# Encoder layer on one core: the first two column groups of each part's down product computed together

## The chip, the cores and the metric

The kernel runs on one core of one Trainium2 chip. The metric is device time in microseconds (us); lower is better. The engines are called as in the profile: PE (TensorE, matmuls), PEld (its weight loads), DVE (VectorE), ACT (ScalarE), POOL (GpSimd) and SP (SyncE, which here only starts DMA transfers).

## What is computed

One layer of an encoder on 256 tokens with model width 2048 and feed-forward width 5632: a feed-forward block, a mixer of three attention-like groups, a second feed-forward block, each between two RMS norms.

```python
def _swiglu(x, w_gate_up, w_down):
    gu = x @ w_gate_up
    g, u = jnp.split(gu, 2, axis=-1)
    return (jax.nn.silu(g) * u) @ w_down
...
    f = _swiglu(_rmsnorm(h, ffn1_norm_pre[l]), ffn1_w_gate_up[l], ffn1_w_down[l])
    h = h + 0.5 * _rmsnorm(f, ffn1_norm_post[l])
    ...
    f = _swiglu(_rmsnorm(h, ffn2_norm_pre[l]), ffn2_w_gate_up[l], ffn2_w_down[l])
    h = h + 0.5 * _rmsnorm(f, ffn2_norm_post[l])
```

## The kernel before

**Numbers.** Everything is fp32. Each operand of a large product is split into a high and a low part (`split_out` for activations, `load_unit` for weights), and the product is made of three matmuls: high by high, high by low, low by high (lines 221 to 223).

**Weights.** `load_unit` brings one block of 512 rows by 512 columns (1 MB) with one DMA on SP's queue into one of three buffers `raw`, and splits it in two units of 256 rows each: ACT writes `whi` (line 209), DVE writes `wlo` (line 210). There are four buffers of each, so a unit can be split at most four units ahead of PE: unit k needs the buffer of unit k-4 back. `mm_unit` multiplies one unit with one token tile (t is 0 or 1, 128 tokens each): 6 matmuls of 128x512, called a step below. A unit is two steps.

**A feed-forward block** (`ffn`) walks over the 11 chunks of 512 hidden columns in three parts of 4, 4 and 3 chunks. For each chunk it computes gate and up (`gemm` over the whole width), then `turn` transposes the product of both. That is a chain of five: the product on DVE (line 319, `th`), a block transpose on DVE (line 165, `blk`), a DMA out to DRAM (line 167, `blkd`), four DMAs back (line 170, `trn`), both started by POOL, and the split into high and low, `h_aT` on ACT (line 133) and `l_aT` on DVE (line 134), for t=0 and then t=1. After the last chunk of a part, `gemm` computes the down product of the part's chunks for each of four groups of 512 columns (oc 0 to 3), and `done` adds it to the rows F. The chunks are used in order, so within oc 0 the chunk that was made last comes last, 12 steps after the end of gate and up in a part of 4 chunks, 8 steps after it in a part of 3. The prediction calls the parts F1-0, F1-1, F1-2 (first block) and F2-0, F2-1, F2-2 (second).

**Side work.** `later(delay, ...)` puts work into a list that is emptied as steps pass (or earlier, when a product needs it): the splits of a chunk come 8 and 9 steps after its `turn`. `beside_down` is called after a column group of the first block. At (1, 0) it loads the memory rows and puts a small product (`spread`, `ps_d`) 8 steps later; in part 2 it loads and splits one piece of the memory, transposed (`rawT`, `h_mT`, `l_mT`), per column group.

**Order.** PE and SP run in the order in which the code is written. On ACT, DVE and POOL a scheduler sets the order when the program is built, and each of these engines then runs its instructions in that fixed order.

Of the kernel before, what the change touches and what calls it, by code (L numbers as in the profile page):

```python
# [9 lines left out]
F32 = mybir.dt.float32  # L10
F32R = mybir.dt.float32r
AF = mybir.ActivationFunctionType
ALU = mybir.AluOpType
# [3 lines left out]
P = 128  # L17
T = 256
NT = T // P
D = 2048  # L20
FF = 5632
CH = 512
KG = 4
# [18 lines left out]
def encoder_layer(ctx: ExitStack, tc: tile.TileContext, x, xt, mem, memt, f1_gu, f1_dn, f2_gu, f2_dn, w_in, w_kv, w_out,  # L42
                  cols, bias, ws_t, rows, out):
    nc = tc.nc
# [11 lines left out]
    psum = ctx.enter_context(tc.tile_pool(name="psum", bufs=8, space=PS))  # L56
# [23 lines left out]
    step = [0]  # L80
# [5 lines left out]
    def run_side(pair=None, t=None):  # L86

        n = sum(1 for e in side if e[0] <= step[0])
        if pair is not None:
            for i, e in enumerate(side):  # L90
                if e[2] is pair and (t is None or e[3] is None or e[3] == t):
                    n = max(n, i + 1)
        for _ in range(n):
            side.pop(0)[1]()
# [101 lines left out]
    def load_unit(w, k0, nk, c0, fine=False):  # L196

        raw = wraw.tile([P, KG, CH], F32, name="raw", tag="raw")
        src = w[c0 // CH, k0 // KG][:, k0 % KG:k0 % KG + nk, :]
        for j in range(0, nk, 1 if fine else nk):  # L200
            e = j + 1 if fine else nk
            nc.sync.dma_start(out=raw[:, j:e, :], in_=src[:, j:e, :])
        got = []
        for j in range(0, nk, 2):
            hi = wsp.tile([P, 2, CH], F32R, name="whi", tag="whi")
            lo = wsp.tile([P, 2, CH], F32R, name="wlo", tag="wlo")
            for i in range(0, 2, 1 if fine else 2):
                a, b = slice(i, i + 1 if fine else 2), slice(j + i, j + i + 1 if fine else j + 2)
                nc.scalar.copy(out=hi[:, a, :], in_=raw[:, b, :])  # L209
                nc.vector.tensor_tensor(out=lo[:, a, :], in0=raw[:, b, :], in1=hi[:, a, :].bitcast(F32), op=ALU.subtract)  # L210
            got.append((hi, lo))
        return got

    def mm_unit(ps, t, pair, half, w, first, last):
        hi, lo = pair
        whi, wlo = w
        ts = slice(t * P, (t + 1) * P)
        for j in range(2):
            kt = 2 * half + j
            f, l = first and j == 0, last and j == 1  # L220
            nc.tensor.matmul(ps, lhsT=hi[:, kt, ts], rhs=whi[:, j, :], start=f, stop=False)  # L221
            nc.tensor.matmul(ps, lhsT=hi[:, kt, ts], rhs=wlo[:, j, :], start=False, stop=False)  # L222
            nc.tensor.matmul(ps, lhsT=lo[:, kt, ts], rhs=whi[:, j, :], start=False, stop=l)  # L223

    def gemm(pairs, w, k0, c0, skew_in=False, skew_out=False, feed=None, nk=KG, done=None):

        ps = [psum.tile([P, CH], F32, name=f"pg{t}", tag="ps") for t in range(NT)]
        n = 2 * len(pairs)  # L230
        units = []
        order = [(u, t) for u in range(n) for t in range(NT)]
        S = min(4, n)
        if skew_in:
            order = [(u, t) for t in range(NT) for u in range(S)] + [(u, t) for u, t in order if u >= S]
        if skew_out:
            order = [(u, t) for u, t in order if u < n - S] + [(u, t) for t in range(NT) for u in range(n - S, n)]
        for u, t in order:
            while len(units) <= u:
                if feed:  # L240
                    feed(len(units))
                units += load_unit(w, k0 + 2 * len(units), nk, c0, nk < KG and len(units) < 2)
            run_side(pairs[u // 2], t)
            mm_unit(ps[t], t, pairs[u // 2], u % 2, units[u], u == 0, u == n - 1)
            if done and u == n - 1:
                done(t, ps[t])
            step[0] += 1
            run_side()
        return ps

    def gemm_T(pairs, w, c0, done):

        ps = [psum.tile([P, CH], F32, name=f"pT{h}", tag="ps")[:, 0:T] for h in range(4)]
        n = 2 * len(pairs)
        units = []
        order = [(u, h) for u in range(n - 2) for h in range(4)] + [(u, h) for h in range(4) for u in (n - 2, n - 1)]
        for i, (u, h) in enumerate(order):
            while len(units) <= u:
                units += load_unit(w, 2 * len(units), KG, c0)
            pair = pairs[u // 2]  # L260
            run_side(pair)
            hi, lo = pair
            whi, wlo = units[u]
            hs = slice(h * P, (h + 1) * P)
            for j in range(2):
                kt = 2 * (u % 2) + j
                f, l = u == 0 and j == 0, u == n - 1 and j == 1
                nc.tensor.matmul(ps[h], lhsT=whi[:, j, hs], rhs=hi[:, kt, :], start=f, stop=False)  # L268
                nc.tensor.matmul(ps[h], lhsT=whi[:, j, hs], rhs=lo[:, kt, :], start=False, stop=False)  # L269
                nc.tensor.matmul(ps[h], lhsT=wlo[:, j, hs], rhs=hi[:, kt, :], start=False, stop=l)  # L270
            if u == n - 1:
                done(h, ps[h])
            if i % 2:
                step[0] += 1
                run_side()
# [9 lines left out]
    def row_scale(src):  # L285

        return [rsqrt_mean(sum_cols(square_sums([src[:, t, q * CH:(q + 1) * CH] for q in range(4)])), D)
                for t in range(NT)]

    def ffn(trn, xT, w_gu, w_dn, F, on_last, feeds=None, beside_down=None):  # L290
        half_r, rr = [], []
        n_ch = FF // CH
        parts = [range(0, 4), range(4, 8), range(8, 11)]
        for ip, part in enumerate(parts):
            aT = []
            for c in part:
                feed_g, feed_u = feeds if c == 0 and feeds else (None, None)
                g = gemm(xT, w_gu, 0, c * CH, skew_in=(c == 0 and not feeds), feed=feed_g, nk=2 if feed_g else KG)
                u = None
                if feed_u:  # L300
                    u = gemm(xT, w_gu, 0, FF + c * CH, feed=feed_u)
                if c == 0:
                    for r in row_scale(H):
                        a = small.tile([P, 1], F32, name="half_r", bufs=4)
                        b = small.tile([P, 1], F32, name="rr2", bufs=4)
                        nc.vector.tensor_scalar_mul(a, r, 0.5)
                        nc.vector.tensor_tensor(out=b, in0=a, in1=r, op=ALU.mult)
                        half_r.append(a)
                        rr.append(b)
                s = []  # L310
                for t in range(NT):
                    th = tmp.tile([P, CH], F32, name="th", tag="tmp")
                    nc.scalar.activation(out=th, in_=g[t], func=AF.Tanh, scale=half_r[t])
                    nc.vector.scalar_tensor_tensor(out=th, in0=th, scalar=1.0, in1=g[t], op0=ALU.add, op1=ALU.mult)
                    s.append(th)
                u = u or gemm(xT, w_gu, 0, FF + c * CH)
                pair = act_pair("aT")
                for t in range(NT):
                    nc.vector.scalar_tensor_tensor(out=s[t], in0=s[t], scalar=rr[t], in1=u[t], op0=ALU.mult,
                                                   op1=ALU.mult)  # L320
                split = turn(trn, s, pair)
                for t in range(NT):
                    later(8 + t, lambda split=split, t=t: split(t), pair, t)
                aT.append(pair)
            last = ip == len(parts) - 1
            for oc in range(4):

                def done(t, d):
                    f = F[t][:, oc * CH:(oc + 1) * CH]

                    def add():
                        nc.vector.tensor_tensor(out=f, in0=f, in1=d, op=ALU.add)

                    if ip == 0:
                        nc.scalar.copy(out=f, in_=d)
                    elif not last:
                        add()
                    else:
                        on_last(oc, t, f, add)

                gemm(aT, w_dn, part[0] * KG, oc * CH, skew_out=last and oc == 3, done=done)
                if beside_down:
                    beside_down(ip, oc)

# [28 lines left out]
    F = token_rows("F")  # L373
# [44 lines left out]
    with tc.tile_pool(name="trn1", bufs=1) as trn:  # L418
        ffn(trn, xT, f1_gu, f1_dn, F, lambda oc, t, f, add: (add(), post[0].piece(oc, t, f)), feeds=(first_xT, first_rows),
            beside_down=memory_T)  # L420
# [370 lines left out]
```

## Time and profile before

| | |
|---|---|
| time, median of 3 runs | 1861.13 us (1861.03, 1861.13, 1865.01) |
| time of the profiled execution | 1863.18 us |
| its span, first to last instruction | 1861.4 us |
| PE busy | 1820.2 us (98%) |
| DVE, ACT, POOL busy | 1077.2, 867.6, 83.3 us |
| DMA moved | 382.35 MB, 205 GB/s over the span |

The rows that follow come from the profiled execution. Busy time of PE is that of overlapping matmuls: one matmul of 128x512 shows as 0.39 us, but the next one starts 0.227 us after it, so distances are read from start to start. "Granted clock" is the share of PE's full speed (2.4 GHz) that the chip allowed; the lower level is 1.2 GHz.

### The profile page before, as it was taken

Reading aid. Unit: us, or ns where it says so; the run is one execution under the profiler, and the core shown is the slowest. Engines: PE = TensorE matmul, PEld = TensorE weight load, DVE = VectorE, ACT = ScalarE, POOL = GpSimd, SP = SyncE. Lnnn points to the kernel's source line nnn. Section 1 sums busy time; section 2 is a strip of 40 time slices with the busy share of each in tenths; the row PEclk is TensorE's granted clock in tenths of the full one; section 3 lists DMA queues with packets and bytes.
Section 4 is the critical chain, followed back from the end, with each engine's and each line's share of the span. In section 5 each row is a group of like instructions: output and inputs, shape, how many; then the busy total and the mean of one; then the engine's idle time right before and its main releaser. Section 6 shows DMA issues by size and latency. Waiting matters only on the chain.

```text
span 1861.4 us, 21799 instructions
## 1 busy us (share of the span) xinstructions
PE 1820.2 (98%) x8662; PEld 1527.8 (82%) x8662; DVE 1077.2 (58%) x1228; ACT 867.6 (47%) x1096; POOL 83.3 (4%) x139
## 2 busy tenths in 40 slices
PE   9999999999999979999999999999999999999986
PEld 7888888888888868999999877888888887888875
DVE  6555445555455556856765776555445555455556
ACT  6444444445344434645454556444444443344444
POOL 0000000000000000000000000001000000000000
PEclk9999999999999989999999999999999999999998
DMA  8666655667556664554554545666556666556652
GB/s 322 242 207 225 204 196 205 224 213 269 182 202 205 239 194 181 204 181 160 208 191 177 191 180 205 210 224 221 205 195 213 221 208 214 194 196 211 224 183 90
DMA packets 63957, 382.35 MB, mean 205 GB/s; under 512 B 8048, under 2 KB 10096, under 8 KB 22256
## 3 DMA queue, kind: packets, MB, share of 16 engines
q1 hardware_dynamic: 51120, 347.10, 52.8%
q0 software_dynamic: 7392, 23.08, 4.5%
q10 hardware_dynamic: 5344, 10.79, 1.7%
q8 instruction: 67, 1.10, 0.2%
q14 instruction: 34, 0.28, 0.0%
HBM read 367.31 MB, written 13.63 MB: 205 GB/s over the span
## 4 chain that ended last, share of the span: by engine, by line
PE 87%; DMA 5%; issue 3%; DVE 3%; ACT 1%; POOL 1%; SPq 0%; POOLq 0%; ACTq 0%; DVEq 0%
PE pg L221 26%; PE pg L223 26%; PE pg L222 26%; PE pT L270 2%; PE pT L268 2%; PE pT L269 2%; DMA trn<-blkd 2%; DMA blkd<-blk 1%; DMA raw<-in_f_gu 1%; DMA memrow<-in_mem 1%; DVE H L369 1%; DVE wlo L210 1%; POOL trn L170 1%; ACT junk L123 1%; ACT whi L209 0%
## 5 line engine op out<-in xcount | busy, mean ns | idle before, releaser
L210 DVE TENSOR_TENSOR wlo<-raw,whi 128x1024 fp32r<-128x1024 f32 (+1 forms) x650 | 791.8, 1220 | 686.5 <-ACT whi L209 685.4
L209 ACT CAST whi<-raw 128x1024 fp32r<-128x1024 f32 (+1 forms) x650 | 681.8, 1050 | 840.3 <-PE pg L223 777.8
L222 PE MATMUL pg<-wlo,h_xT 128*128 128x512 f32 x1408 | 548.8, 390 | 2.2 <-DVE wlo L210 2.2
L221 PE MATMUL pg<-whi,h_xT 128*128 128x512 f32 x1408 | 549.1, 390 | 0.9 <-ACT h_xT L133 0.8
L223 PE MATMUL pg<-whi,l_xT 128*128 128x512 f32 x1408 | 548.3, 389 | 0.5 <-DVE l_xT L134 0.5
L222 PEld LDWEIGHTS pg<-wlo,h_xT 128*128 128x128 f32 x1408 | 264.4, 188 | 59.3 <-DVE wlo L210 4.4
L221 PEld LDWEIGHTS pg<-whi,h_xT 128*128 128x128 f32 x1408 | 264.4, 188 | 56.5 <-ACT whi L209 1.3
L223 PEld LDWEIGHTS pg<-whi,l_xT 128*128 128x128 f32 x1408 | 264.4, 188 | 56.3 <-DVE l_xT L134 1.3
L221 PE MATMUL pg<-whi,h_aT 128*128 128x512 f32 x704 | 276.4, 393 | 18.4 <-ACT h_aT L133 18.4
L223 PE MATMUL pg<-whi,l_aT 128*128 128x512 f32 x704 | 275.6, 391 | 0.0
L222 PE MATMUL pg<-wlo,h_aT 128*128 128x512 f32 x704 | 275.5, 391 | 0.0
L221 PEld LDWEIGHTS pg<-whi,h_aT 128*128 128x128 f32 x704 | 133.1, 189 | 47.7 <-ACT h_aT L133 20.5
L223 PEld LDWEIGHTS pg<-whi,l_aT 128*128 128x128 f32 x704 | 133.0, 189 | 29.7 <-DVE l_aT L134 2.0
L222 PEld LDWEIGHTS pg<-wlo,h_aT 128*128 128x128 f32 x704 | 133.1, 189 | 27.5
L268 PE MATMUL pT<-h_hT,whi 128*128 128x256 f32 x320 | 91.0, 284 | 0.0
L270 PE MATMUL pT<-h_hT,wlo 128*128 128x256 f32 x320 | 90.5, 283 | 0.0
L269 PE MATMUL pT<-l_hT,whi 128*128 128x256 f32 x320 | 90.5, 283 | 0.0
L167 POOL DMA_DIRECT2D blkd<-blk x22 | 12.9, 587 | 1096.4 <-DVE blk L165 1070.3
L269 PEld LDWEIGHTS pT<-l_hT,whi 128*128 128x128 f32 x320 | 61.4, 192 | 0.2
L268 PEld LDWEIGHTS pT<-h_hT,whi 128*128 128x128 f32 x320 | 61.4, 192 | 0.2
L270 PEld LDWEIGHTS pT<-h_hT,wlo 128*128 128x128 f32 x320 | 61.4, 192 | 0.0
L170 POOL DMA_DIRECT2D trn<-blkd x88 | 53.0, 631 | 86.8 <-DMA blkd<-blk 65.5
(160 smaller groups left out, 1252.3 us busy)
## 6 DMA issues: line engine op xcount, KB each, us to landing
raw<-in_f_gu SPq DMA_DIRECT2D x172, 1024.0 KB, 4.8
raw<-in_f_dn SPq DMA_DIRECT2D x88, 1024.0 KB, 4.8
raw<-in_w_in SPq DMA_DIRECT2D x36, 1024.0 KB, 4.8
raw<-in_w_out SPq DMA_DIRECT2D x16, 1024.0 KB, 4.9
blkd<-blk POOLq DMA_DIRECT2D x22, 512.0 KB, 3.3
trn<-blkd POOLq DMA_DIRECT2D x88, 128.0 KB, 5.5
raw<-in_w_kv SPq DMA_DIRECT2D x8, 1024.0 KB, 4.8
grow<-in_rows ACTq DMA_DIRECT2D x4, 1024.0 KB, 6.0
```

What stands on the lines that cost most here:

```text
L123: nc.scalar.activation(out=junk, in_=src, func=AF.Square, accum_out=acc)
L167: nc.gpsimd.dma_start(out=d, in_=b)
L170: nc.gpsimd.dma_start(out=c[q * B:(q + 1) * B].rearrange("i t (a c) -> i t a c", a=KG), in_=d[:, :, q * P:(q + 1) * P].rearrange("(a i) t ...
L209: nc.scalar.copy(out=hi[:, a, :], in_=raw[:, b, :])
L210: nc.vector.tensor_tensor(out=lo[:, a, :], in0=raw[:, b, :], in1=hi[:, a, :].bitcast(F32), op=ALU.subtract)
L221: nc.tensor.matmul(ps, lhsT=hi[:, kt, ts], rhs=whi[:, j, :], start=f, stop=False)
L222: nc.tensor.matmul(ps, lhsT=hi[:, kt, ts], rhs=wlo[:, j, :], start=False, stop=False)
L223: nc.tensor.matmul(ps, lhsT=lo[:, kt, ts], rhs=whi[:, j, :], start=False, stop=l)
L268: nc.tensor.matmul(ps[h], lhsT=whi[:, j, hs], rhs=hi[:, kt, :], start=f, stop=False)
L269: nc.tensor.matmul(ps[h], lhsT=whi[:, j, hs], rhs=lo[:, kt, :], start=False, stop=False)
L270: nc.tensor.matmul(ps[h], lhsT=wlo[:, j, hs], rhs=hi[:, kt, :], start=False, stop=l)
L369: nc.vector.scalar_tensor_tensor(out=H[:, t, c], in0=self.f[t, q], scalar=self.r[t], in1=H[:, t, c], op0=ALU.mult, op1=ALU.add)
```

## The change

A new function `gemm_pair` computes the down products of column groups 0 and 1 together, in four PSUM tiles (two column groups by two token tiles). It goes through all chunks but the last for group 0, through all but the last for group 1, then through the last chunk for group 0 and for group 1. Groups 2 and 3 stay as they were. `beside_down(ip, 0)` and `(ip, 1)` are both called after the pair. The number of instructions of each kind stays the same.

```diff
--- before.py
+++ after.py
@@ -247,6 +247,22 @@
             step[0] += 1
             run_side()
         return ps
+
+    def gemm_pair(pairs, w, k0, cols, done):
+
+        ps = [[psum.tile([P, CH], F32, name=f"pg{t}", tag="ps") for t in range(NT)] for _ in cols]
+        n = 2 * len(pairs)
+        for us in (range(0, n - 2, 2), range(n - 2, n, 2)):
+            for g, c0 in enumerate(cols):
+                for u0 in us:
+                    for u, unit in enumerate(load_unit(w, k0 + 2 * u0, KG, c0), u0):
+                        for t in range(NT):
+                            run_side(pairs[u // 2], t)
+                            mm_unit(ps[g][t], t, pairs[u // 2], u % 2, unit, u == 0, u == n - 1)
+                            if u == n - 1:
+                                done(g, t, ps[g][t])
+                            step[0] += 1
+                            run_side()
 
     def gemm_T(pairs, w, c0, done):
 
@@ -323,22 +339,27 @@
                     later(8 + t, lambda split=split, t=t: split(t), pair, t)
                 aT.append(pair)
             last = ip == len(parts) - 1
-            for oc in range(4):
-
-                def done(t, d):
-                    f = F[t][:, oc * CH:(oc + 1) * CH]
-
-                    def add():
-                        nc.vector.tensor_tensor(out=f, in0=f, in1=d, op=ALU.add)
-
-                    if ip == 0:
-                        nc.scalar.copy(out=f, in_=d)
-                    elif not last:
-                        add()
-                    else:
-                        on_last(oc, t, f, add)
-
-                gemm(aT, w_dn, part[0] * KG, oc * CH, skew_out=last and oc == 3, done=done)
+
+            def done(oc, t, d):
+                f = F[t][:, oc * CH:(oc + 1) * CH]
+
+                def add():
+                    nc.vector.tensor_tensor(out=f, in0=f, in1=d, op=ALU.add)
+
+                if ip == 0:
+                    nc.scalar.copy(out=f, in_=d)
+                elif not last:
+                    add()
+                else:
+                    on_last(oc, t, f, add)
+
+            gemm_pair(aT, w_dn, part[0] * KG, (0, CH), done)
+            if beside_down:
+                beside_down(ip, 0)
+                beside_down(ip, 1)
+            for oc in (2, 3):
+                gemm(aT, w_dn, part[0] * KG, oc * CH, skew_out=last and oc == 3,
+                     done=lambda t, d, oc=oc: done(oc, t, d))
                 if beside_down:
                     beside_down(ip, oc)
 
```

The first place is **PE in part F1-0**, at the point where all but the last chunk have been used for column group 0. In a name like `h_aT_1416` the number tells buffers apart: 516, 816 and 1116 (low parts 517, 817, 1117) are the first three chunks of the part, 1416 the last; `pg0_1430` and `pg1_1431` are group 0's PSUM tiles, `pg0_1432` and `pg1_1433` group 1's. Before:

```order
L221 MATMUL pg1_1431<-whi_1508,h_aT_1116 128x512
L222 MATMUL pg1_1431<-wlo_1509,h_aT_1116 128x512
L223 MATMUL pg1_1431<-whi_1508,l_aT_1117 128x512
L221 MATMUL pg0_1430<-whi_1540,h_aT_1416 128x512
L222 MATMUL pg0_1430<-wlo_1541,h_aT_1416 128x512
L223 MATMUL pg0_1430<-whi_1540,l_aT_1417 128x512
```

With the change:

```order
L221 MATMUL pg1_1431<-whi_1510,h_aT_1116 128x512
L222 MATMUL pg1_1431<-wlo_1511,h_aT_1116 128x512
L223 MATMUL pg1_1431<-whi_1510,l_aT_1117 128x512
L221 MATMUL pg0_1432<-whi_1542,h_aT_516 128x512
L222 MATMUL pg0_1432<-wlo_1543,h_aT_516 128x512
L223 MATMUL pg0_1432<-whi_1542,l_aT_517 128x512
```

The last chunk's first use moved from 72 matmuls behind the start of the down product to 144 behind it (in a part of 3 chunks from 48 to 96).

The second place is **ACT in part F1-2**, around the split of the last chunk (`h_aT_4692`). The two `whi` of one `raw` are two units; in both kernels 4708 or 4710 holds units 0 and 1, 4778 or 4780 units 4 and 5. Before (4838 holds units 6 and 7, 4872 units 8 and 9):

```order
L209 CAST whi_4840<-raw_4838 128x1024
L209 CAST whi_4844<-raw_4838 128x1024
L133 CAST h_aT_4692<-trn_4701 128x4x128 x2
L133 CAST h_mT_4822<-rawT_4824 128x512
L133 CAST h_mT_4822<-rawT_4830 128x512
L133 CAST h_mT_4948<-rawT_4950 128x512
L133 CAST h_mT_4948<-rawT_4956 128x512
L133 CAST h_mT_5074<-rawT_5076 128x512
L133 CAST h_mT_5074<-rawT_5082 128x512
L133 CAST h_mT_5200<-rawT_5202 128x512
L184 DMA rawT_5208<-in_memt 128x512
L209 CAST whi_4874<-raw_4872 128x1024
```

With the change (4850 holds units 8 and 9, 4892 units 10 and 11):

```order
L209 CAST whi_4852<-raw_4850 128x1024
L133 CAST h_aT_4692<-trn_4701 128x4x128 x2
L133 CAST h_mT_4934<-rawT_4936 128x512
L133 CAST h_mT_4934<-rawT_4942 128x512
L209 CAST whi_4856<-raw_4850 128x1024
L133 CAST h_mT_4948<-rawT_4950 128x512
L133 CAST h_mT_4948<-rawT_4956 128x512
L133 CAST h_mT_5074<-rawT_5076 128x512
L209 CAST whi_4894<-raw_4892 128x1024
L133 CAST h_mT_5074<-rawT_5082 128x512
L133 CAST h_mT_5200<-rawT_5202 128x512
L184 DMA rawT_5208<-in_memt 128x512
```

The split of the last chunk stands one unit later than before, behind unit 8, and the splits of the memory pieces, which stood in one run before the next unit, now stand in groups before units 9, 10 and 11.

The third place is **DVE in the same part**, from the last weight unit ahead of the last chunk's low part. Before:

```order
L210 TENSOR_TENSOR wlo_4845<-raw_4838,whi_4844 128x1024
L134 TENSOR_TENSOR l_aT_4693<-trn_4701,h_aT_4692 128x4x128 x2
L134 TENSOR_TENSOR l_mT_4823<-rawT_4824,h_mT_4822 128x512
L134 TENSOR_TENSOR l_mT_4823<-rawT_4830,h_mT_4822 128x512
L134 TENSOR_TENSOR l_mT_4949<-rawT_4950,h_mT_4948 128x512
L134 TENSOR_TENSOR l_mT_4949<-rawT_4956,h_mT_4948 128x512
L134 TENSOR_TENSOR l_mT_5075<-rawT_5076,h_mT_5074 128x512
L134 TENSOR_TENSOR l_mT_5075<-rawT_5082,h_mT_5074 128x512
L134 TENSOR_TENSOR l_mT_5201<-rawT_5202,h_mT_5200 128x512
L210 TENSOR_TENSOR wlo_4875<-raw_4872,whi_4874 128x1024
```

With the change:

```order
L210 TENSOR_TENSOR wlo_4853<-raw_4850,whi_4852 128x1024
L134 TENSOR_TENSOR l_aT_4693<-trn_4701,h_aT_4692 128x4x128 x2
L134 TENSOR_TENSOR l_mT_4935<-rawT_4936,h_mT_4934 128x512
L134 TENSOR_TENSOR l_mT_4935<-rawT_4942,h_mT_4934 128x512
L210 TENSOR_TENSOR wlo_4857<-raw_4850,whi_4856 128x1024
L134 TENSOR_TENSOR l_mT_4949<-rawT_4950,h_mT_4948 128x512
L134 TENSOR_TENSOR l_mT_4949<-rawT_4956,h_mT_4948 128x512
L210 TENSOR_TENSOR wlo_4895<-raw_4892,whi_4894 128x1024
L134 TENSOR_TENSOR l_mT_5075<-rawT_5076,h_mT_5074 128x512
L134 TENSOR_TENSOR l_mT_5075<-rawT_5082,h_mT_5074 128x512
L134 TENSOR_TENSOR l_mT_5201<-rawT_5202,h_mT_5200 128x512
L210 TENSOR_TENSOR wlo_4899<-raw_4892,whi_4898 128x1024
```

The order is that of ACT: two, two and three low parts of the memory pieces stand ahead of the low parts of units 9, 10 and 11. In the parts of 4 chunks the split of the last chunk keeps its place, behind unit 8 and ahead of unit 9.

## Rows read from the trace of the kernel before

**Rows 1.** The page: span, PE's busy time, and granted clock in 40 slices (tenths).

```profile
span 1861.4 us, 21799 instructions
...
PE 1820.2 (98%) x8662; PEld 1527.8 (82%) x8662; DVE 1077.2 (58%) x1228; ACT 867.6 (47%) x1096; POOL 83.3 (4%) x139
...
PEclk9999999999999989999999999999999999999998
```

**Rows 2.** PE's waits on the last chunk: us in total, times, longest us.

```profile
PE pg L221 <- ACT h_aT L133: 18.4, 5, 11.4
```

**Rows 3.** Timeline of PE, part F1-0: start us, duration us, instruction, [idle before].

```profile
184.59 0.39 PE L221 MATMUL pg<-whi,h_aT 128*128 128x512 f32 x1
...
200.69 0.39 PE L223 MATMUL pg<-whi,l_aT 128*128 128x512 f32 x1
...
202.84 0.40 PE L221 MATMUL pg<-whi,h_aT 128*128 128x512 f32 x1
```

**Rows 4.** Timeline of PE, around the waits in F1-1 and F2-1.

```profile
463.07 0.39 PE L223 MATMUL pg<-whi,l_aT 128*128 128x512 f32 x1
...
464.71 0.40 PE L221 MATMUL pg<-whi,h_aT 128*128 128x512 f32 x1
...
1569.84 0.39 PE L223 MATMUL pg<-whi,l_aT 128*128 128x512 f32 x1
...
1572.21 0.39 PE L221 MATMUL pg<-whi,h_aT 128*128 128x512 f32 x1
```

**Rows 5.** Timeline of PE, around the wait in F1-2.

```profile
676.47 0.39 PE L223 MATMUL pg<-whi,l_aT 128*128 128x512 f32 x1
...
688.30 0.79 PE L221 MATMUL pg<-whi,h_aT 128*128 128x512 f32 x1 [11.44 <-ACT h_aT L133]
...
693.45 0.40 PE L221 MATMUL pg<-whi,h_aT 128*128 128x512 f32 x1
```

**Rows 6.** Timeline of PE, around the wait in F2-2.

```profile
1783.49 0.39 PE L223 MATMUL pg<-whi,l_aT 128*128 128x512 f32 x1
...
1789.01 0.79 PE L221 MATMUL pg<-whi,h_aT 128*128 128x512 f32 x1 [5.13 <-ACT h_aT L133]
...
1792.50 0.39 PE L223 MATMUL pg<-whi,l_aT 128*128 128x512 f32 x1
```

**Rows 7.** Windows of F1-2: busy us by engine, then granted clock, DMA share, GB/s.

```profile
677.00:688.00 11.00, 0.00 (x0) 0.00 (x0) 1.23 (x1) 1.31 (x2) 2.33 (x4) 0.62 0.76 209
688.00:693.50 5.50, 5.20 (x13) 4.05 (x14) 5.22 (x9) 4.40 (x9) 0.00 (x0) 0.52 0.14 49
```

**Rows 8.** Timelines of POOL, ACT and DVE in F1-2.

```profile
668.43 0.58 POOL L167 DMA_DIRECT2D blkd<-blk  x1 [37.28 <-DVE blk L165]
...
676.92 2.41 POOL L170 DMA_DIRECT2D trn<-blkd  x4 [7.91 <-DMA blkd<-blk]
...
676.89 1.04 ACT L209 CAST whi<-raw 128x1024 fp32r<-128x1024 f32 x1 [1.62 <-PE pg L223]
...
687.63 1.14 ACT L133 CAST h_aT<-trn 128x512 fp32r<-128x512 f32 x2 [9.69 <-DMA trn<-blkd]
...
688.67 1.65 ACT L133 CAST h_mT<-rawT 128x512 fp32r<-128x512 f32 x3
...
677.97 1.23 DVE L210 TENSOR_TENSOR wlo<-raw,whi 128x1024 fp32r<-128x1024 f32 x1 [1.44 <-ACT whi L209]
...
688.28 1.29 DVE L134 TENSOR_TENSOR l_aT<-trn,h_aT 128x512 fp32r<-128x512 f32 x2 [9.08 <-ACT h_aT L133]
...
689.49 4.30 DVE L134 TENSOR_TENSOR l_mT<-rawT,h_mT 128x512 fp32r<-128x512 f32 x7
```

**Rows 9.** Timeline of ACT: the last chunk's split in F2-1 and F2-2.

```profile
1570.48 1.14 ACT L133 CAST h_aT<-trn 128x512 fp32r<-128x512 f32 x2 [1.88 <-DMA trn<-blkd]
...
1788.34 1.14 ACT L133 CAST h_aT<-trn 128x512 fp32r<-128x512 f32 x2 [3.38 <-DMA trn<-blkd]
```

**Rows 10.** Windows, columns as in Rows 7: 128x256 matmuls over four open PSUM tiles.

```profile
749.50:757.50 8.00, 8.00 (x69) 8.00 (x69) 7.56 (x11) 5.52 (x12) 1.46 (x1) 1.00 0.99 386
```

## The prediction

> **What bounds the kernel now.** I read the page first. PE is busy for 1820.2 of 1861.4 us, and the granted clock is at 9 tenths or more in all but two slices, of which one is the 15th of 40 (651 to 698 us, with the start of F1-2's down product in it) and the other the last [rows 1]. So PE is the bound nearly everywhere, and a change that neither adds nor removes matmuls can only win or lose in PE's pauses and in the stretches at the lower clock. The table of PE's waits came second. Nearly all of what PE waits for has one cause, the split of a part's last chunk: 18.4 us in five waits, the longest 11.4 us [rows 2]. Third I went to the timeline of PE at each of these waits and measured the whole loss from start to start, because what is lost is more than the idle time.
>
> The pitch without a wait: from the first to the 72nd matmul of the down product in F1-0 there are 71 distances in 200.69 - 184.59 = 16.10 us, 0.2268 us each [rows 3]. A step of 6 matmuls is then 1.36 us, a unit 2.72 us. The loss of each wait is the distance from the last matmul ahead of it to the first one back in rhythm, less the pitch of the matmuls between:
> - F1-0: 202.84 - 200.69 = 2.15, less 4 pitches (0.91): 1.24 us [rows 3]
> - F1-1: 464.71 - 463.07 = 1.64, less 0.91: 0.73 us [rows 4]
> - F2-1: 1572.21 - 1569.84 = 2.37, less 0.91: 1.46 us [rows 4]
> - F1-2: 693.45 - 676.47 = 16.98, less 13 pitches (2.95): 14.03 us [rows 5]
> - F2-2: 1792.50 - 1783.49 = 9.01, less 9 pitches (2.04): 6.97 us [rows 6]
>
> Together 24.4 us; F2-0 has no such wait. The two parts of 3 chunks make 21.0 of it. In F1-2, 688.30 - 676.47 - 0.23 = 11.6 us are the wait itself, and 2.4 us follow it: the 12 matmuls from 688.30 to 693.45 start 0.43 us apart in place of 0.23 [rows 5], and the window shows a granted clock of 0.52, the lower of the two levels, behind a stretch in which PE ran nothing [rows 7]. F2-2 has the same on a smaller scale, 5.3 and 1.7 us.
>
> **What the change removes.** It lets PE do 72 or 48 matmuls more before the last chunk is needed: 144 matmuls (32.7 us) after the start of the down product in a part of 4, 96 (21.8 us) in a part of 3. Against this stands when the split really comes. I count from the start of the down product, found by going back from the last matmul ahead of the wait (71 or 47 pitches).
> - Parts of 4: the latest is F2-1. It starts at 1569.84 - 16.10 = 1553.74, and the split starts at 1570.48 [rows 9], 16.7 us in. Wanted at 32.7: 16 us to spare. The whole loss goes, 1.24 + 0.73 + 1.46 = 3.4 us.
> - F2-2: start 1783.49 - 10.66 = 1772.83, split at 1788.34 [rows 9], 15.5 us in, wanted at 21.8: 6 us to spare. 6.97 us go.
> - F1-2: start 676.47 - 10.66 = 665.81. The split starts at 687.63, and PE's first matmul with it at 688.30, 22.5 us in [rows 5, 8]. Wanted at 21.8. So here a wait of 0.7 us stays. The chain is slow in this part: between the DMA out at 668.43 and the DMAs back at 676.92 lie 8.5 us, of which POOL waits 7.9 [rows 8]. Nothing that the change touches runs ahead of 676.47, and from there to the split the same transfers are queued, since ACT stands at the split and frees no further `raw`; so I let the chain end where it did.
>
> **What is late next.** ACT and DVE keep a fixed order, and the split waits on them ahead of later weight units. In the parts of 4 it stands between units 8 and 9. In F2-1 ACT would be through with it at 16.7 + 1.14, `whi` of unit 9 takes 1.04 and its `wlo` 1.23 [rows 8, 9]: ready 20.2 us in. PE reaches unit 9 after 108 matmuls, 24.5 us in. So 4 us of cover are left, and a later split would cost PE from there on what it is late, no matter that the chunk itself is wanted only at 32.7. In F2-2 (15.5 us in) there is more.
>
> F1-2 has no such cover, and the memory pieces stand in the way as well. On ACT an `h_mT` takes 1.65 / 3 = 0.55 us, on DVE an `l_mT` 4.30 / 7 = 0.61 us [rows 8]. With the split where it was:
> - third matmul of unit 8: half of `l_aT` is done at 688.28 + 0.65 = 688.93, wanted at 688.75; I take 0.3 us with the loads behind it
> - unit 9: ACT 688.67 + 2 x 0.55 + 1.04 = 690.8; DVE behind two `l_mT` and 1.23 of its own 692.05; PE wants it at 665.81 + 108 pitches + 1.0 + 0.23 = 691.5: 0.5 us late
> - unit 10: DVE 694.75, PE wants it at 694.77: just in time
> - unit 11: DVE 694.75 + 3 x 0.61 + 1.23 = 697.8, wanted at 697.5: 0.3 us late
>
> So F1-2 keeps 0.7 + 0.3 + 0.5 + 0.3 = 1.8 us of its 14.0. The pauses are short ones, like those of the parts of 4, after which the matmuls were back at full pitch within four [rows 3, 4], so I add nothing for the clock.
>
> **What I cost at nothing.** Matmuls, weight blocks, POOL's and SP's instructions stay the same in number. The two groups' adds (and in the last parts the gains behind them) come closer together: eight operations of 128x512, some 0.65 us each as half of `l_aT` [rows 8], 5.2 us, beside four `wlo` (4.9 us), in four units of PE (10.9 us). DVE holds that with little to spare; what covers it is that the units are split up to four ahead. If that cover is gone, as it may be in F1-2 behind the late split, it costs up to 2 us. The four open PSUM tiles instead of two: see the third rival. The memory's side product moves by one column group, with its inputs ready as before.
>
> **Sum.** 24.4 - 1.8 = 22.6 us. The profiled execution took 1863.18 us (1861.4 of it its span), which gives 1840.6. The median of the runs is 2.05 us lower. The waits end with DMA landings, which is what may differ between runs: if the 2 us lie there, the new kernel has 1840.6 in every run; if elsewhere, 1838.6. I take 1839.8, and the bounds: all 24.4 gone on the lower runs 1836.7; a split in F1-2 that is later by as much as F1-2 is behind F2-2 today (22 - 15.5 = 6.5 us) 1847.1.
>
> **Rivals.**
> 1. *The wait moves to the weights behind the split.* If the split comes later with PE running on (the DMAs back now share their time with busy matmuls), F1-2 pays each us in full, and units 9 to 11 stack up behind it. For it: ACT and DVE stand still in front of the split today, with 1.3 and 1.2 us of work in 11 [rows 7]. Against it: the weights wanted in that time are split already. [...] 3 to 9 us: 1843 to 1850. Chance 0.11.
> 2. *Nothing is gained*, because something else fills the pauses, DMA above all: its engines are 0.76 busy in the pause of F1-2 [rows 7]. Then PE would wait for `whi` or `wlo` instead. But these waits would have to be as long as the old ones, and a unit, on which PE works 2.72 us, costs ACT and DVE only 1.04 and 1.23 us [rows 8]. 1858 to 1864. Chance 0.03.
> 3. *Slower: the clock falls while four PSUM tiles are open.* The place is the pair, 4 x 192 + 2 x 144 = 1056 matmuls. At the lower level each costs 0.20 us more [rows 5], 211 us if all did; from 113 of them on (11%) the gain of 22.6 us is gone, and from 131 on the kernel is measurably slower, 1865 us or more. Against it: today's transposed products go round four open tiles, 69 matmuls of half the width in 8.00 us, 0.116 us each, at a granted clock of 1.00 [rows 10], and the pair changes between two tiles at a time as before. Chance 0.03. The Trainium skill speaks for this rival (TensorE: Matmul & The Clock Gate, "A second HAM failure mode: psum-queue depth-cycling"): cycling through PSUM banks made TensorE pause so often between groups of matmuls that its clock went back and forth between the levels. This trace has no sign of it with four tiles; by that rule the sum would be a loss, by the row it is nothing.
>
> **How the numbers follow.** The forecast, 1836.5 to 1843, has 0.80. Rival 1 has 0.11, rivals 2 and 3 have 0.03 each, and 0.03 is left for a time below 1836.5, if PE gains more than its waits. The range goes from 1836 to 1847: it holds the forecast and the nearer half of rival 1. A measurement of this kernel can tell about 0.2% (3.7 us) from no change. Faster than that are the forecast, what lies below it and rival 1, 0.94; same 0.03; slower 0.03.
>
> **What would show it.** PE's waits on the last chunk's split are gone but for some 1 us in F1-2. There `whi` and `wlo` of units 9 and 11 appear as new waits of under 1 us each. The granted clock is full in the 15th slice. In F2-1 the split still starts some 17 us into the down product, and unit 9 is split by 20 us. The prediction is wrong if the split of F1-2 starts more than 25 us into the down product, if PE waits for weights in the parts of 4, or if matmuls of the pair start more than 0.23 us apart.

## The result and the profile after

The changed kernel takes 1839.34 us (median of 4 runs, 1838.24 to 1840.51), the kernel before 1862.51 us on the same chip (4 runs, 1861.03 to 1865.01). The ratio is 0.9874, 95% interval 0.9857 to 0.9891: 1.26% faster. The profiled executions took 1863.18 us before and 1840.51 us after, 22.7 us apart.

The page after the change, with the same three rows as in [rows 1]:

```profile
span 1838.7 us, 21801 instructions
...
PE 1815.0 (99%) x8662; PEld 1526.4 (83%) x8662; DVE 1076.3 (59%) x1228; ACT 866.3 (47%) x1096; POOL 83.5 (5%) x139
...
PEclk9999999999999999999999999999999999999998
```

PE is busy for 5.2 us less (most of it the matmuls at the lower clock, which were longer), in a span that is 22.7 us shorter, and the granted clock no longer drops in the 15th slice. All of PE's waits after the change (us in total, times, longest us):

```profile
PE pg L222 <- DVE wlo L210: 2.2, 5, 0.8
PE pt L144 <- DVE H L390: 1.9, 2, 1.0
PE warm_ps L75 <- POOL ones L62: 1.1, 1, 1.1
PE pg L221 <- ACT whi L209: 0.8, 1, 0.8
PE pg L221 <- ACT h_xT L133: 0.8, 1, 0.8
PE pg L223 <- DVE l_xT L134: 0.4, 1, 0.4
PE pT L286 <- DVE wlo L210: 0.2, 1, 0.2
```

The row of [rows 2] has no counterpart: nothing on PE waits for `h_aT` by this table. What is left is old work at the start of the kernel and between the blocks, and one new piece, which the timeline of PE in F1-2 shows (start us, duration us, instruction, [idle before]; to be read beside [rows 5]):

```profile
686.04 0.39 PE L223 MATMUL pg<-whi,l_aT 128*128 128x512 f32 x1
686.57 0.50 PE L221 MATMUL pg<-whi,h_aT 128*128 128x512 f32 x1
686.91 0.40 PE L222 MATMUL pg<-wlo,h_aT 128*128 128x512 f32 x1
687.30 0.50 PE L223 MATMUL pg<-whi,l_aT 128*128 128x512 f32 x1
687.64 0.40 PE L221 MATMUL pg<-whi,h_aT 128*128 128x512 f32 x1
...
689.70 0.39 PE L221 MATMUL pg<-whi,h_aT 128*128 128x512 f32 x1
690.36 0.50 PE L222 MATMUL pg<-wlo,h_aT 128*128 128x512 f32 x1 [0.27 <-DVE wlo L210]
690.70 0.40 PE L223 MATMUL pg<-whi,l_aT 128*128 128x512 f32 x1
```

The distance from 686.04 to 686.57 is 0.53 us, one pitch (0.23) and 0.30 of waiting for the split; the three matmuls that follow are 0.39 late together. The distance from 689.70 to 690.36 is 0.66, a wait of 0.43 for `wlo` of unit 9, with 0.11 behind it. These are all distances above the pitch in F1-2: 1.23 us, where [rows 5] had 14.03. The other five parts have none, and over the pair of each part the granted clock is 1.00. The timelines of POOL, ACT and DVE in F1-2, beside [rows 8]:

```profile
667.13 0.58 POOL L167 DMA_DIRECT2D blkd<-blk  x1 [37.26 <-DVE blk L165]
...
675.88 2.41 POOL L170 DMA_DIRECT2D trn<-blkd  x4 [8.18 <-DMA blkd<-blk]
...
685.90 1.14 ACT L133 CAST h_aT<-trn 128x512 fp32r<-128x512 f32 x2 [6.54 <-DMA trn<-blkd]
...
687.99 1.05 ACT L209 CAST whi<-raw 128x1024 fp32r<-128x1024 f32 x1
...
686.55 1.29 DVE L134 TENSOR_TENSOR l_aT<-trn,h_aT 128x512 fp32r<-128x512 f32 x2 [5.93 <-ACT h_aT L133]
...
687.76 1.29 DVE L134 TENSOR_TENSOR l_mT<-rawT,h_mT 128x512 fp32r<-128x512 f32 x2
...
689.08 1.23 DVE L210 TENSOR_TENSOR wlo<-raw,whi 128x1024 fp32r<-128x1024 f32 x1
```

The down product starts at 686.04 - 95 pitches = 664.5. The DMA out is issued 2.6 us in, the DMAs back 11.4 us in, the split starts 21.4 us in; before it was 2.6, 11.1 and 21.8. The chain is what it was, and PE has other work while it runs. In the two parts that [rows 9] show, the split starts at:

```profile
1555.89 1.14 ACT L133 CAST h_aT<-trn 128x512 fp32r<-128x512 f32 x2 [1.52 <-DMA trn<-blkd]
...
1774.56 1.14 ACT L133 CAST h_aT<-trn 128x512 fp32r<-128x512 f32 x2 [2.59 <-DMA trn<-blkd]
```

F2-1 starts at 1539.5 (2.6 us ahead of its DMA out) and F2-2 at 1757.1: 16.4 and 17.4 us in, and wanted at 32.7 and 21.8.

### The profile page after: what moved, and what is told of

Same layout as the page of the kernel before. It is cut to its first block, busy times and chain, and to the rows that moved or that the text cites. A ratio compares the mean times of both kernels' runs of the same rounds, so it can differ in the third digit from the quotient of the medians.

```text
span 1838.7 us, 21801 instructions
## 1 busy us (share of the span) xinstructions
PE 1815.0 (99%) x8662; PEld 1526.4 (83%) x8662; DVE 1076.3 (59%) x1228; ACT 866.3 (47%) x1096; POOL 83.5 (5%) x139
## 4 chain that ended last, share of the span: by engine, by line
PE 93%; DVE 2%; DMA 2%; ACT 1%; POOL 0%; issue 0%; SPq 0%; ACTq 0%; POOLq 0%
PE pg L222 28%; PE pg L223 28%; PE pg L221 28%; PE pT L286 2%; PE pT L284 2%; PE pT L285 2%; DMA raw<-in_f_gu 1%; DVE H L390 1%; DVE wlo L210 1%; DMA H<-in_x 1%; DMA trn<-blkd 0%; DMA blkd<-blk 0%; ACT whi L209 0%; ACT junk L123 0%; PE ps_p L528 0%
```

## Experiments

For each run I give the loss in the six down products, measured start to start as in the prediction (24.5 us in the profiled execution before, with 0.1 us in F2-0). The time of an execution less this loss should be the same number for every kernel with the same work, if these losses are all that differs.

### The pair in the parts of 3 chunks only

```diff
-            gemm_pair(aT, w_dn, part[0] * KG, (0, CH), done)
+            paired = len(part) == 3
+            if paired:
+                gemm_pair(aT, w_dn, part[0] * KG, (0, CH), done)
...
-            for oc in (2, 3):
+            for oc in range(2 if paired else 0, 4):
```

> The pair stands in the two parts of 3 chunks only; the parts of 4 are as before. Theory (the gain is the sum of the removed losses, part by part): F1-2 and F2-2 give 14.0 + 7.0 - 1.2 = 19.8 us, so about 1842.7 us on runs of before at 1862.5, and PE's waits in F1-0, F1-1 and F2-1 are back with 0.2 to 1 us each. Rival (the pair gains by something general, such as a steadier clock or fewer column-group changes, in proportion to the 1056 matmuls in it): 288 of 1056 matmuls, 6 us, about 1856 us.

Measured: 1846.26 us (1844.45 to 1848.83, 4 runs) against 1862.79 for the kernel before (17 runs), ratio 0.9904 (0.9888 to 0.9921). That is 16.5 us, not 19.8, and far from the 6 of the rival. The profiled execution (1848.83 us, the slowest of the four) shows F1-2 and F2-2 without loss and where gain is missing: F1-1 lost 7.6 us, ten times what it lost before, F2-1 1.9, F2-0 0.4. PE's waits in F1-1, and ACT, DVE and POOL there:

```profile
PE pg L221 <- ACT h_aT L133: 5.2, 1, 5.2
...
446.91 0.63 ACT L123 ACTIVATE junk<-memrow 128x512 f32<-128x512 f32 x1 [3.20 <-DMA memrow<-in_mem]
...
447.67 0.16 DVE L111 TENSOR_REDUCE ssum<-ssp 128x1 f32<-128x4 f32 x1 [4.08 <-ACT junk L123]
...
448.88 0.74 DVE L335 SCALAR_TENSOR_TENSOR th<-th,rr,pg 128x512 f32<-128x512 f32 x1
...
451.33 1.30 DVE L165 STREAM_TRANSPOSE blk<-th 128x512 f32<-128x512 f32 x2
...
452.93 0.62 POOL L167 DMA_DIRECT2D blkd<-blk  x1 [4.28 <-DVE blk L165]
...
456.83 2.42 POOL L170 DMA_DIRECT2D trn<-blkd  x4 [3.29 <-DMA blkd<-blk]
...
467.12 1.14 ACT L133 CAST h_aT<-trn 128x512 fp32r<-128x512 f32 x2 [6.21 <-DMA trn<-blkd]
```

On DVE the sum of the memory rows (`ssum`, with `rv` and `dg`) stands ahead of the last chunk's product `th`. It waits for ACT's square of the last memory row at 446.91, and that for the row's DMA. So `blk` comes at 451.33 and the DMA out at 452.93, 6.9 us into the down product (which starts at 446.06), against 3.4 us before (450.40 and 446.98); the DMAs back take 10.3 us to the split, 8.7 before. DVE's order is the same in the kernel before, only that the row was there in time:

```profile
444.39 0.63 ACT L123 ACTIVATE junk<-memrow 128x512 f32<-128x512 f32 x1
...
445.15 0.16 DVE L111 TENSOR_REDUCE ssum<-ssp 128x1 f32<-128x4 f32 x1 [0.59 <-ACT junk L123]
...
446.36 0.74 DVE L319 SCALAR_TENSOR_TENSOR th<-th,rr,pg 128x512 f32<-128x512 f32 x1
```

There the last square ran 2.6 us ahead of the start of the down product, here 0.9 us behind it. So 3.5 of the 5.1 us by which the split is later come from a memory row that landed late, which DVE's order passes on to the last chunk. Why the row and the DMAs back took longer, the trace doesn't tell. A part of 4 without the pair has 12 steps (16.3 us) of cover, which such an execution overruns; with the pair it has 24.

### The pair in the parts of 4 chunks only

The same edit with `paired = len(part) == 4`.

> The pair stands in the four parts of 4 chunks only. Theory: 3.4 us gained, about 1859 us; the waits of 11 and 5 us in F1-2 and F2-2 are there, each with its stretch at the lower clock. With the run that has the pair in the parts of 3 the two gains add up to that of the whole change (23 us). Rival (general gain): 768 of 1056 matmuls, 17 us, about 1845 us.

Measured: 1858.74 us (1856.47 to 1863.11, 8 runs), ratio 0.9979 (0.9966 to 0.9991), 4.0 us. PE's waits on the split are two, 15.1 us together (10.2 and 4.9), and the loss is 19.3 us, all in F1-2 and F2-2. The two gains add up to 20.6 us, the whole change gave 23.2: within what the spread of the kernel before allows (1857 to 1868 in these 17 runs). The rival, a gain in proportion to the matmuls in the pair, is out: 768 of them give 4 us, 288 give 16.5.

### Four tiles, but the old order of products

```diff
-        for us in (range(0, n - 2, 2), range(n - 2, n, 2)):
+        for us in (range(0, n, 2),):
```

> The pair keeps its four PSUM tiles and the two calls of the memory work behind it, but goes through all chunks for group 0 and then through all for group 1, so PE's order of products is that of before. Theory: no gain, the time of before within 3 us (1859 to 1866 us), waits on the last chunk's split of 11 and 5 us. Rival (four open tiles, or the moved memory work, are part of the gain): half of the gain or more stays, 1851 us or less; if they cost something by themselves, more than 1866 us.

Measured: 1861.44 us (1858.83 to 1868.78, 10 runs), ratio 0.9992 (0.9977 to 1.0006). PE's waits on the split are back (us in total, times, longest us):

```profile
PE pg L221 <- ACT h_aT L133: 20.5, 5, 10.0
```

The profiled execution (1868.78 us) was the slowest of the ten; it lost 29.5 us in the down products, 6.6 of them in F1-1, where the DMA out was issued 5.9 us in, behind a late memory row as in the run with the pair in the parts of 3. Four open PSUM tiles and the moved memory work neither give nor cost anything that can be told. The gain lies in the order of the products alone.

### The memory pieces of F1-2 loaded later, from SP's queue

```diff
-                load_T(memt, oc, memT[oc], C_MEM, half, nc.scalar, r_mem)
+                load_T(memt, oc, memT[oc], C_MEM, half, nc.sync, r_mem)
```

> The changed kernel, but the memory pieces of the first block's part 2 are loaded from SP's queue, in order behind the pair's weights, not from ACT's queue at the time of the last chunk's DMA to DRAM. Theory (that DMA is slow in F1-2 because these loads share the DMA engines with it): the DMA out and the wait of POOL shrink from 8.2 to some 3 to 4 us, the split starts 16 to 18 us into the down product instead of 21.4, and the 0.7 us of that wait go; with the memory pieces later, the 0.5 us at unit 9 go as well: 1 us less than the changed kernel, which only the profile can tell. Rival (the DMA is slow for the weights' sake): the split starts at 21 us as before. A risk of its own: SP stands at a memory load whose buffer is not free, and weights behind it come late.

Measured: 1838.89 us (1838.49 to 1839.56, 4 runs), ratio 0.9868 (0.9854 to 0.9883). POOL and ACT in F1-2:

```profile
666.15 0.57 POOL L167 DMA_DIRECT2D blkd<-blk  x1 [37.22 <-DVE blk L165]
...
670.16 2.41 POOL L170 DMA_DIRECT2D trn<-blkd  x4 [3.43 <-DMA blkd<-blk]
...
680.25 1.14 ACT L133 CAST h_aT<-trn 128x512 fp32r<-128x512 f32 x2 [1.86 <-DMA trn<-blkd]
```

The DMA out, 8.75 us from its issue to that of the DMAs back in the changed kernel, takes 4.0, and the split starts 16.7 us into the down product (663.5) instead of 21.4. F1-2 has no loss left, and all six parts together 0.2 us (0.1 of it the small product). So the slow chain of F1-2 was made by the memory pieces' loads, which ACT issues just ahead of the DMA out (667.58 and 668.43 in the kernel before); the weights' loads at that time are the same in both kernels, 2.9 us ahead of the start of the down product and 3.5 us behind it. In time this is the changed kernel (1839.34) within what can be measured.

### Three column groups together in the parts of 3

```diff
-            gemm_pair(aT, w_dn, part[0] * KG, (0, CH), done)
+            m = 3 if len(part) == 3 else 2
+            gemm_pair(aT, w_dn, part[0] * KG, [oc * CH for oc in range(m)], done)
...
-            for oc in (2, 3):
+            for oc in range(m, 4):
```

> The changed kernel, but in the parts of 3 chunks three column groups are computed together (six PSUM tiles): the last chunk is wanted after 144 matmuls, 32.7 us, instead of 21.8. Theory: the wait on the split in F1-2 (0.7 us) goes; the late low part of unit 9 goes too, if the weight units behind the split have more time, or stays at 0.4 us, since the split still stands ahead of unit 9 on ACT and DVE; 0.3 to 1.2 us less than the changed kernel in the profile, the same within 2 us in time. Rival (six open tiles are too many beside those of gate and up): PE waits for PSUM, 1842 us or more.

Measured: 1839.22 us (1837.50 to 1840.77, 4 runs), ratio 0.9874 (0.9849 to 0.9898), the changed kernel's time. The split of F1-2 is no longer waited for. What is left there is 0.98 us, 24.5 us into the down product, where unit 9 begins: its `wlo` is late by 0.88, because it stands behind the split and two pieces of the memory on ACT and DVE. More cover for the split itself does not buy this back.

### A longer chain, in both kernels

Two more copies from DRAM to DRAM between the DMA out and the DMAs back, in every chunk.

```diff
         nc.gpsimd.dma_start(out=d, in_=b)
+        for i in range(2):
+            d2 = scratch.tile([P, NT, CH], F32, name="hop", tag=f"hop{i}")
+            nc.gpsimd.dma_start(out=d2, in_=d)
+            d = d2
```

In the kernel before:

> The kernel before, with two more copies from DRAM to DRAM in the chain of every chunk (the DMA out is copied twice before the four DMAs back), so that the last chunk's split comes later by some 4 us per copy. Theory (PE waits for the end of the chain, and each us later is a us lost): six waits, each some 8 us longer than before, and five or six stretches at the lower clock at 2 us: 1863 + 6 x 8 + 4 x 2 = about 1920 us. Rival (the chain has cover that the profile does not show): under 1890 us.

In the changed kernel:

> The changed kernel with the same two copies. Theory (the pair gives 10.9 us more cover in a part of 3 chunks and 16.3 us in a part of 4): the parts of 4 take 16 to 17 us + 8 us against 32.7 wanted and lose nothing, or up to 2 us where the split holds up the weight units behind it; F2-2 (15.5 + 8 against 21.8) loses 2 to 3 us; F1-2 (21.4 + 8) loses 8 us and a stretch at the lower clock. About 1839 + 13 = 1852 us, some 68 us less than the kernel before with the copies. Rival (the gain is a fixed amount, not cover): 23 us less than the kernel before with the copies, about 1897 us.

Measured: 1943.09 us for the kernel before with the copies (2 runs, ratio to the kernel before 1.0428, 1.0386 to 1.0471), 1875.72 us for the changed kernel with them (8 runs, 1.0074, 1.0054 to 1.0094). The difference is 67.4 us, as expected (68), not the 23 of a fixed gain. Both absolute times came out 23 and 24 us above what I expected, for two reasons. The two copies cost more than 8 us. From the DMA out to the split the chains of the kernel before took 12.5 to 19.2 us, with the copies 20.7 to 25.5: 6.3 to 12.4 us more, 9.3 on average. In F1-1 the DMA out was issued 4.4 us later as well. With the stretches at the lower clock, which now stand behind all six waits, the six parts lost 90.2 us, where the expectation comes to 80.5 (24.5 + 6 x 8 + 4 x 2). The other reason stands in PE's waits, of the kernel before with the copies and of the changed one with them:

```profile
PE pg L225 <- ACT h_aT L133: 77.5, 6, 17.7
PE pg L225 <- ACT whi L213: 6.3, 6, 2.4
PE pg L226 <- DVE wlo L214: 5.7, 9, 0.8
```

```profile
PE pg L225 <- ACT h_aT L133: 11.5, 2, 6.7
PE pg L226 <- DVE wlo L214: 8.6, 14, 0.8
PE pg L225 <- ACT whi L213: 2.2, 5, 0.7
```

In the changed kernel `wlo` is waited for 14 times, 8.6 us, against 5 times and 2.2 us without the copies, nearly all of it in gate and up. The splits of the earlier chunks stand ahead of weight units on ACT and DVE, and when they come late, the units behind them do. From start to start and from 50 us on, gate and up lost 18.5 us in the kernel before with the copies and 13.2 us in the changed one, against 1.7 us in both without. In the down products the changed kernel lost 18.2 us: 9.2 in F1-2, 6.95 in F2-2 and 2.0 in F1-1 on weights behind the split; F1-0, F2-0 and F2-1 lost nothing, though their splits started 25.2 to 26.4 us in, later than unit 9 is wanted (24.5). The reason is that the order on ACT is another one here: two more weight units stand ahead of the split than in the changed kernel, so the next in line is unit 11, wanted 29.9 us in. F1-1, with its split 28.6 us in, lost its 2.0 us just there. How much cover stands behind the split is thus a matter of each program's order, too.

The match with the expected 68 us is in part luck. The profiled execution before was the slower of its two (1947.49 us), the one after the fastest of its eight (1869.04 us). They lie 78.5 us apart, of which the down products make 72.0 and gate and up 5.3. That the gain grows with the chain, 67 us and not 23, holds either way.

### Matmuls that fill a wait

In the kernel before, 20 matmuls of 128x512 in front of the last chunk in F2-2, whose result nobody reads.

```diff
+            if fill and (u, t) == (n - 2, 0):
+                idle = psum.tile([P, CH], F32, name="idle", tag="ps")
+                for i in range(fill):
+                    nc.tensor.matmul(idle.rearrange("p (j n) -> p j n", j=2), lhsT=pairs[0][0][:, 0, 0:P],
+                                     rhs=pairs[0][0][:, 0:2, :], start=True, stop=True)
             run_side(pairs[u // 2], t)
```

> The kernel before, with 20 matmuls of 128x512 whose result nobody reads, put on PE in the second block's part 2 between the last matmul that it can do and the first that needs the last chunk's split (some 4.5 of the 5.3 us of the wait). Theory (the slow matmuls behind the wait are at the lower clock because PE was idle): the wait ends at the same place, and the matmuls behind it start 0.23 us apart at a granted clock of 1.00; 1.7 us of F2-2's 7.0 are gone. Rival (they are slow because what they read comes late, low parts and second token tile): they stay 0.43 us apart.

Measured: 1861.63 us (one run, which says nothing beside the spread of the kernel before; the trace does). The timeline of PE around the wait, and a window of it (busy us of PE, PEld, DVE, ACT and POOL, granted clock, DMA share, GB/s):

```profile
1783.37 4.70 PE L246 MATMUL idle<-h_aT 128*128 128x512 f32 x20
1788.73 0.50 PE L221 MATMUL pg<-whi,h_aT 128*128 128x512 f32 x1 [0.66 <-ACT h_aT L133]
1789.07 0.39 PE L222 MATMUL pg<-wlo,h_aT 128*128 128x512 f32 x1
1789.46 0.50 PE L223 MATMUL pg<-whi,l_aT 128*128 128x512 f32 x1
1789.79 0.39 PE L221 MATMUL pg<-whi,h_aT 128*128 128x512 f32 x1
...
1791.86 0.39 PE L221 MATMUL pg<-whi,h_aT 128*128 128x512 f32 x1
```

```profile
1788.00:1793.00 5.00, 4.34 (x19) 3.23 (x19) 1.29 (x2) 2.08 (x3) 0.00 (x0) 1.00 0.41 174
```

Behind the wait the matmuls start 0.23 us apart, but for 0.38 us in the first three distances, and the granted clock of the window is 1.00. From the first filled matmul to the real ones in rhythm 5.5 us are lost, where [rows 6] had 7.0. In F1-2 of the same execution, where nothing was filled in, a dozen matmuls behind the wait are 0.2 us late each, as in [rows 5]. So the slow matmuls behind a long wait are PE's lower clock after idling, and not operands that come late; they belong to the wait and go with it.

### The memory rows of F1-1 from SP's queue, with the pair in the parts of 3

```diff
-                nc.scalar.dma_start(out=m[c], in_=mem[t * P:(t + 1) * P, c * CH:(c + 1) * CH])
+                nc.sync.dma_start(out=m[c], in_=mem[t * P:(t + 1) * P, c * CH:(c + 1) * CH])
```

> The kernel with the pair in the parts of 3 chunks only, and the eight loads of memory rows moved from ACT's queue to SP's, in code order behind the first column group's weights of F1-1. Theory (in the run without this move, F1-1 lost 7.6 us and not 0.7 because DVE's fixed order puts the sums of the memory rows ahead of the last chunk's product, and one row tile landed 4 us late): the sums now stand behind the transpose of the last chunk, the DMA out starts some 3.5 us into the down product, F1-1 loses under 2 us, and the time is about 1843 us instead of 1846. Rival (F1-1's loss there has another cause, such as slow DMAs back): F1-1 still loses 5 us or more, 1846 us or above. A risk of its own: the rows take SP's queue for 2 MB, and the weights behind them or the small product on PE come late.

Measured: 1851.50 us (1849.01 to 1852.96, 6 runs), ratio 0.9956 (0.9942 to 0.9969). F1-1 lost 10.4 us, more than without the move: 8.4 at the split, and 2.0 at unit 8, whose `wlo` now stands behind the rows' sums on DVE. POOL and ACT in F1-1:

```profile
449.14 0.58 POOL L167 DMA_DIRECT2D blkd<-blk  x1 [37.23 <-DVE blk L165]
...
455.70 2.41 POOL L170 DMA_DIRECT2D trn<-blkd  x4 [5.99 <-DMA blkd<-blk]
...
468.87 1.14 ACT L133 CAST h_aT<-trn 128x512 fp32r<-128x512 f32 x2 [10.21 <-DMA trn<-blkd]
```

The first half of the theory held: DVE came to the last chunk at once, and the DMA out was issued at 449.14, 2.6 us into the down product (446.5). But the memory rows now run beside it: the DMA out takes 6.6 us to the next issue and the DMAs back 13.2 us to the split, which starts 22.4 us in. So I removed one lateness and made another by the same loads. How much of F1-1's loss in the first experiment DVE's order made stays what its trace shows; this run missed both numbers of the theory (under 2 us, and 1843 us) and met those of the rival (5 us or more, 1846 us or above), but with a slowness of the DMAs that the move itself brought, so it doesn't settle it.

## Why the prediction was right

The forecast was 1839.8 us, measured 1839.34; 22.6 us between the profiled executions, measured 22.7.

- *The losses of the parts of 4 go (3.4 us).* Right: none of the four has a distance above the pitch. Alone they gave 4.0 us.
- *F2-2's 7.0 us go.* Right, though the split came 1.9 us later in the part than in the execution before.
- *F1-2 keeps 1.8 of 14.0 us.* Right in kind, 1.23 in size: 0.30 for the split (0.7 expected, the chain ended 0.4 us earlier), 0.39 behind it (0.3), 0.54 at unit 9 (0.5), nothing at unit 11 (0.3).
- *The chain of F1-2 ends where it did.* Right, 21.4 against 21.8 us; the loads that make it slow were shown to be the memory pieces.
- *The stretch at the lower clock belongs to the wait.* Right, by the filled wait.
- *The 2 us between the profiled execution and the median.* Still open, though the losses explain most of what differs between executions. Execution time less loss is 1838.7 for the kernel before, 1839.2 for the changed one, and 1838.8, 1839.7, 1839.3, 1838.3 and 1836.4 for the runs with the pair in the parts of 3, in the parts of 4, with tiles only, with late memory pieces and with three groups. The run with the filled wait gives 1839.6, the one with the memory rows on SP's queue 1839.4. These nine lie within 3.3 us, the executions themselves between 1837.5 and 1868.8. Only the two with the copies stand apart, 1850.8 and 1857.3, by the weights that they wait for elsewhere. So executions with the old waits differ by what these waits come to, and this is the likely reason why the kernel before varied from 1857 to 1870 us over all runs while the changed kernel's four runs lie within 2.3 us; of the kernel before itself I have the losses of only one execution. The forecast took a value between the two ends, 1840.6 and 1838.6. The median lies between them too, and that it lies within half a us of the forecast is luck.
- *Rivals.* The wait that moves to the weights is there, with 0.5 us at unit 9; it grows as soon as the chain does (8.6 us of waiting for `wlo` over the whole kernel with the copies). With the copies the order of ACT had changed as well, so the two are not told apart there. Something else that fills the pauses: no, what PE stopped waiting for came off the time. The clock with four open tiles: no, by the run with tiles only. With that the rule of the Trainium skill that I weighed (TensorE: Matmul & The Clock Gate, "A second HAM failure mode: psum-queue depth-cycling") had no effect here: the window from 664 to 686 us, the first of the pair in F1-2, has 98 matmuls at a granted clock of 1.00.

```profile
664.00:686.00 22.00, 22.00 (x98) 18.22 (x98) 11.56 (x15) 6.42 (x7) 2.99 (x5) 1.00 0.78 247
```

What I had not seen is how uneven the wait of F1-1 is. It showed as 0.73 us in the execution that I read; in other kernels with the old order there it was 1.6, 6.6 and 7.6 us. One execution gave the right sum, since the median lay near it, but a part that had nearly no slack was priced as if its wait were a constant. The forecast of the time stands this, because it takes the losses off the time of the same execution; the gain depends on which executions of the kernel before it is held against.

## What to carry to other kernels

When the last operand of a group comes through a long chain, don't shorten the chain first: reorder independent products so that the others stand in front of it, and compare the time at which the operand is there with that at which it is wanted, part by part. Behind it look for the next thing in line: on engines with a fixed order the step that waits for the operand also holds up what stands behind it, so cover has to be counted for that too. A long wait costs more than its idle time, because the matmuls behind it may run at the lower clock (here 1.7 and 2.4 us behind waits of 5 and 11).

## What the runs showed of the hardware

Two copies of 512 KB from DRAM to DRAM, put in a chain one behind the other, made it 6.3 to 12.4 us longer in the six parts of the kernel before. The same DMA of 512 KB to DRAM took 4.0 us to the next issue with only the weights beside it, and 8.5 and 8.75 us where two loads of 256 KB were issued from another queue just ahead of it. Behind PE's waits of 5.1 and 11.4 us the matmuls ran at the lower of the two levels, and behind a wait of 5 us that 20 idle matmuls filled but for 0.7 us at the full one. Over all traces a slow stretch stood behind each of eighteen waits of 4.4 to 17.9 us; it was 7 to 14 matmuls long and cost 1.4 to 3.0 us, and no longer behind the longer waits.
